# Exponent rows of the SSD heads by broadcast transfers instead of selection matmuls, with the clipped differences pinned in ScalarE's queue

## The chip, the core and the metric

The kernel runs on one core of a Trainium2 chip. Five engines work from queues of their own, each in the order in which its instructions were written: PE (TensorE, matmuls), DVE (VectorE), ACT (ScalarE), POOL (GpSimd) and SP (SyncE, which here only issues transfers). The metric is the device time of one execution in microseconds (us).

## The reference

A two-layer encoder on 512 tokens plus 16 meta tokens (L = 528 positions), width 2048, float32. The even layer is the one that matters here. Its input projection feeds 32 state-space (SSD) heads of width 64 in 8 groups, run forwards and backwards in chunks, and a convolution branch with 31 taps; both are gated and projected out. The odd layer is neighbourhood attention.

```
A_cs = jnp.cumsum(A, axis=2)
seg = A_cs[:, :, :, None] - A_cs[:, :, None, :]
Lmat = jnp.exp(jnp.where(tri, seg, -jnp.inf))
Y_diag = jnp.einsum("bclsgr,bcsgrp->bclgrp", CB[..., None] * Lmat, X)
Y_off = jnp.einsum("bclgn,bcgrpn->bclgrp", Cc, prev) * jnp.exp(A_cs)[..., None]
```

Per head and direction this needs, for every pair of positions in a chunk, the exponential of a difference of cumulative log decays, and for every position the exponential of the cumulative sum itself. The decays never exceed one, so the kernel writes the difference as the negative of a clipped one: exp(-relu(column - row)).

## The kernel before, in words

Positions lie along the free dimension and channels over the 128 partitions. A projection is 96 matmuls of 128x128 by 264 columns: 16 slices of the weights, three products (a high part and a low part of weights and of activations), two column halves. Weights come in halves of a panel, 512 KB each: SP issues the transfer (`raw`, three buffers), ACT splits off the high part (`wh`, L263, three buffers), DVE the low part (`wl`, L266), and PE uses the pair for 48 matmuls (L310). PE walks through the halves in a fixed order, so `wh` of a half can be written once PE has done with the half three back.

The even layer goes over 8 groups `g`. For each there are one or two convolution tiles (`glu_tile`), then six projections for B, C, two tiles of x and two of z. The SSD work of a group is a generator, `ssd`, which the loop pumps between the projections of the next group. Within `ssd` there are two passes `i`, each for two heads `j`:

- `T` (88 x 2 x 528, tag of two buffers) holds the clipped differences, then their exponentials (L611), then those times dt (L618) and times C·B (L619); the two directions are added at L621.
- `cq` (128 x 2 x 528, two buffers) holds the exponentials of the cumulative sums, then those times C (L612, L613).
- 64 matmuls into `py` (L640) read both `T` and both `cq` of the pass; DVE then makes the output y (L644, L645), and POOL writes it out (`yz_d`, L646).

To get one head's row of sums onto all partitions, PE multiplies a broadcast column of a selection matrix `sel` with `fhl`, the sums in a high and a low half (L605, two matmuls per head and direction into `pf` in PSUM). ACT reads `pf` six times for the clipped differences, one per chunk, with the chunk's column of sums as bias (L608), and once for the exponentials (L610). `pf`, `pc` and `py` share one PSUM slot of two banks (tag `big`).

A scheduler with a model of the engines' times places all instructions on the engines' queues; the `yield` numbers in `ssd` are costs that `step` takes off a budget of `SB_` = 7000 per step, and so set where in the program a piece of `ssd` is written.

Of the kernel before, what the change touches and what calls it, by code (L numbers as in the profile page):

```python
# [17 lines left out]
P = 128  # L18
# [65 lines left out]
def hybrid_encoder(ctx: ExitStack, tc: tile.TileContext, hT, win, wdt, wout, oin, oout, par, con,  # L84
# [24 lines left out]
    def cn(n):  # L109
        lo, hi = CON[n]  # L110
        return cst[:, lo:hi]
# [4 lines left out]
    def h2(ap):  # L116
        return ap.rearrange("p (a b) -> p a b", a=2)
# [2 lines left out]
        return h2(ap)[:, :, NB:]  # L120

    yz_d = dr.tile([KT, P, L], F32, name="yz_d")
    cv_d = dr.tile([KT, P, L], F32, name="cv_d")
    pt_d = dr.tile([KT, P, L], F32, name="pt_d")
    yb_d = dr.tile([KT, P, L], F32, name="yb_d")
# [255 lines left out]
    with ExitStack() as c0:  # L381
# [37 lines left out]
                if k >= 2:  # L419
                    nc.vector.tensor_tensor(ac, ac, raw, op=ALU.add)  # L420

        sel = cp.tile([P, 64], F32R, name="sel")
        nc.vector.tensor_copy(sel, cn("sel"))
        xp = [sp.tile([P, L + 4], F32, name=f"xp{i}") for i in range(2)]
        for t in xp:
            nc.gpsimd.memset(t[:, 0:2], 0.0)
# [93 lines left out]
        nc.gpsimd.memset(rf[:, ::CH], 0.0)  # L520
        nc.vector.tensor_tensor_scan(fc[0:32], rf[0:32], la[0:32], 0.0, ALU.mult, ALU.add)
        nc.vector.tensor_tensor_scan(fc[32:64, ::-1], rf[32:64], la[32:64, ::-1], 0.0, ALU.mult, ALU.add)
        fhl = dp.tile([P, L], F32R, name="fhl")
        nc.scalar.activation(fhl[:J], fc, AF.Copy)
        nc.vector.tensor_tensor(fhl[J:], fc, fhl[:J].bitcast(F32), op=ALU.subtract)
        fc3 = fc.rearrange("p (c t) -> p c t", c=NC)
        wd3 = wd.rearrange("p (c t) -> p c t", c=NC)
        nc.vector.tensor_tensor(wd3[0:32], fc3[0:32, :, CH - 1:CH].to_broadcast([32, NC, CH]), fc3[0:32], op=ALU.subtract)
# [20 lines left out]
            cols.append(t)  # L549
        fcol, dcol, wcol = cols  # L550

        def ssd(g, bT, cT, xs, zs):
            xb = sp.tile([CH, NC, 3 * P], F32, name="xb", tag="xb")
            pv = sp.tile([P, NC - 1, 2, 256], F32, name="pv", tag="pv")
            pc = psb.tile([P, 2, 512], F32, name="pc", tag="big")
# [38 lines left out]
            for i in range(2):  # L594
                gs, cs = [], []
                for j in range(2):
                    hl = 2 * i + j
                    hd = HPG * g + hl
                    T = sp.tile([CH, 2, L], F32, name="T", tag="T", bufs=2)
                    cq = sp.tile([P, 2, L], F32, name="cq", tag="cq", bufs=2)  # L600
                    for d in range(2):
                        pf = psb.tile([P, 2, 512], F32, name="pf", tag="big")
                        jj = d * NH + hd
                        for n in range(2):
                            nc.tensor.matmul(pf[:, n, :HL], sel[:, jj:jj + 1].to_broadcast([P, P]),  # L605
                                             fhl[:, n * HL:(n + 1) * HL], start=True, stop=True)
                        for c in range(NC):
                            nc.scalar.activation(T[:, d, c * CH:(c + 1) * CH], pf[:CH, c // 3, (c % 3) * CH:(c % 3 + 1) * CH],  # L608
                                                 AF.Relu, bias=fcol[:, c, d, hd:hd + 1], scale=-1.0)
                        nc.scalar.activation(h2(cq[:, d]), pf[:, :, :HL], AF.Exp)  # L610
                    nc.scalar.activation(T, T, AF.Exp, scale=-1.0)  # L611
                    nc.vector.tensor_tensor(cq[:, 0, CH:], cq[:, 0, CH:], cT[:, CH:], op=ALU.mult)  # L612
                    nc.vector.tensor_tensor(cq[:, 1, :L - CH], cq[:, 1, :L - CH], cT[:, :L - CH], op=ALU.mult)  # L613
                    yield 1050
                    for d in range(2):
                        for c in range(NC):
                            sl = slice(c * CH, (c + 1) * CH)
                            nc.scalar.activation(T[:, d, sl], T[:, d, sl], AF.Copy, scale=dcol[:, c, d, hd:hd + 1])  # L618
                        nc.vector.tensor_tensor(T[:, d], T[:, d], cbs[d], op=ALU.mult)  # L619
                    yield 1900  # L620
                    nc.vector.tensor_tensor(T[:, 0], T[:, 0], T[:, 1], op=ALU.add)  # L621
                    yield 650
                    gs.append(T)
                    cs.append(cq)
                py = psb.tile([P, 2, 512], F32, name="py", tag="big")
                for c in range(NC):
                    sl = slice(c * CH, (c + 1) * CH)
                    terms = [[], []]
                    for j in range(2):
                        hs = slice((2 * i + j) * HD, (2 * i + j + 1) * HD)  # L630
                        terms[j].append((xb[:, c, hs], gs[j][:, 0, sl]))
                        if c > 0:
                            terms[j].append((pv[:, c - 1, 0, hs], cs[j][:, 0, sl]))
                        if c < NC - 1:
                            terms[j].append((pv[:, NC - 2 - c, 1, hs], cs[j][:, 1, sl]))
                    nt = len(terms[0])
                    for q in range(nt):
                        for j in range(2):
                            a, b = terms[j][q]
                            nc.tensor.matmul(py[j * HD:(j + 1) * HD, c // 3, (c % 3) * CH:(c % 3 + 1) * CH], a, b,  # L640
                                             start=(q == 0), stop=(q == nt - 1))
                ti = 2 * g + i
                y = xs[i]
                nc.vector.scalar_tensor_tensor(h2(y), h2(y), pr("dd", ti, ti + 1), py[:, :, :HL], op0=ALU.mult, op1=ALU.add)  # L644
# [4 lines left out]
                else:  # L649
                    nc.scalar.activation(zs[i], y, AF.Square)  # L650
                    nc.vector.tensor_tensor(accy, accy, zs[i], op=ALU.add)
                yield 2100

        def step():
            pump(bgs, SB_)
# [974 lines left out]
```

## Time and profile before

| | |
|---|---|
| time, median of 3 runs | 2628.63 us (2628.37 to 2631.36) |
| profiled execution | 2629.41 us, span 2627.6 us |
| granted TensorE clock | 0.998 |
| SSD stretch in the span | about 140 to 1065 us |
| `pf` matmuls (L605) | 128 |
| `T` from `pf` on ACT (L608) | 384 |
| `cq` from `pf` on ACT (L610) | 64 |

The span runs from the first to the last instruction of the profiled execution. A busy PE in the page is not by itself a PE without gaps, since matmuls overlap; the distance from one start to the next tells more.

### The profile page before, as it was taken

How to read it: one execution, taken by the hardware profiler on the slowest of the kernel's cores; microseconds unless marked ns; L12 is line 12 of the kernel's file. 1: busy time of each engine (PE TensorE's matmuls, PEld its weight loads, DVE VectorE, ACT ScalarE, POOL GpSimd, SP SyncE). 2: the span in 40 equal slices, each digit the busy share in tenths (PEclk: the TensorE clock that was granted, in tenths of full speed). 3: DMA queues.
4: the chain of work that ended last, by engine and by line, in shares of the span. 5: the costliest groups of instructions: out<-in, count | busy, mean ns of one | idle time of the engine just before them, and what ended most of it. 6: DMA issues, size and time to landing. Idle time of an engine off the chain costs nothing.

```text
span 2627.6 us, 52699 instructions
## 1 busy us (share of the span) xinstructions
PE 2593.7 (99%) x21236; PEld 2480.7 (94%) x21236; DVE 2044.7 (78%) x3073; ACT 1421.8 (54%) x2654; POOL 335.8 (13%) x561
## 2 busy tenths in 40 slices
PE   8999999999999999999999999999999999999997
PEld 8999999999999999999999999999999987777797
DVE  6985967887686969997788888877777776666887
ACT  5366585666558566325554566644334355556543
POOL 0000000000000001100210311300000043434110
PEclk9999999999999999999999999999999999999999
DMA  4322223222222222533875876755555555544665
GB/s 174 100 74 94 81 77 95 82 95 73 94 85 74 89 91 90 175 107 104 274 231 164 300 219 208 258 161 161 156 161 146 151 143 139 135 120 130 224 186 159
DMA packets 163173, 373.28 MB, mean 142 GB/s; under 512 B 40896, under 2 KB 70784, under 8 KB 162928
## 3 DMA queue, kind: packets, MB, share of 16 engines
q1 hardware_dynamic: 137840, 289.96, 34.5%
q0 software_dynamic: 23072, 78.30, 11.2%
q8 instruction: 167, 2.74, 0.4%
q10 hardware_dynamic: 2016, 1.65, 0.2%
q14 instruction: 78, 0.64, 0.1%
HBM read 320.59 MB, written 49.25 MB: 141 GB/s over the span
## 4 chain that ended last, share of the span: by engine, by line
PE 87%; DVE 4%; ACT 4%; DMA 3%; issue 2%; POOL 0%; SPq 0%; DVEq 0%; ACTq 0%; POOLq 0%
PE ps L310 43%; PE pb L287 29%; PE ps L1192 6%; PE py L640 2%; PE po L1178 1%; PE st L580 1%; DVE a L454 1%; PE pq L1129 1%; DMA srt<-yb_d 1%; ACT T L608 1%; ACT L610 1%; DVE wl L266 1%; PE pa L1153 1%; DMA wy<-oout 1%; ACT wh L263 1%
## 5 line engine op out<-in xcount | busy, mean ns | idle before, releaser
L310 PE MATMUL ps<-rh,wh 128*128 128x264 f32 (+2 forms) x3520 | 730.3, 287 | 10.0 <-ACT rh L327 8.0
L310 PE MATMUL ps<-rh,wl 128*128 128x264 f32 (+2 forms) x3520 | 730.2, 287 | 0.0
L310 PE MATMUL ps<-rl,wh 128*128 128x264 f32 (+2 forms) x3520 | 725.6, 287 | 0.7 <-DVE rl L328 0.6
L263 ACT ACTIVATE wh<-raw 128x1024 fp32r<-128x1024 f32 (+1 forms) x349 | 368.9, 1057 | 525.3 <-PE ps L310 271.3
L310 PEld LDWEIGHTS ps<-rh,wh 128*128 128x128 f32 (+1 forms) x3520 | 549.2, 188 | 16.1 <-ACT rh L327 8.6
L266 DVE TENSOR_TENSOR wl<-raw,wh 128x1024 fp32r<-128x1024 f32 (+1 forms) x349 | 436.5, 1251 | 163.2 <-ACT wh L263 158.4
L310 PEld LDWEIGHTS ps<-rh,wl 128*128 128x128 f32 (+1 forms) x3520 | 548.9, 188 | 2.3 <-DVE wl L266 0.3
L310 PEld LDWEIGHTS ps<-rl,wh 128*128 128x128 f32 (+1 forms) x3520 | 546.5, 188 | 4.1 <-DVE rl L328 1.5
L287 PE MATMUL pb<-rh,wh 128*128 128x264 f32 (+1 forms) x1280 | 363.1, 284 | 3.3 <-DVE fo L1494 1.2
L287 PE MATMUL pb<-rl,wh 128*128 128x264 f32 (+1 forms) x1280 | 362.2, 283 | 0.0
L287 PE MATMUL pb<-rh,wl 128*128 128x264 f32 (+1 forms) x1280 | 361.8, 283 | 0.3 <-DVE wl L266 0.2
L454 DVE SCALAR_TENSOR_TENSOR a<-up,prm,a 128x528 f32<-128x528 f32 x464 | 342.9, 769 | 2.3 <-ACT a L449 0.9
L287 PEld LDWEIGHTS pb<-rh,wh 128*128 128x128 f32 x1280 | 241.1, 188 | 4.4 <-issue 1.7
L287 PEld LDWEIGHTS pb<-rh,wl 128*128 128x128 f32 x1280 | 240.3, 188 | 0.7 <-DVE wl L266 0.7
L287 PEld LDWEIGHTS pb<-rl,wh 128*128 128x128 f32 x1280 | 240.7, 188 | 0.0
L287 PE MATMUL pb<-ta,wh 128*128 128x264 f32 (+1 forms) x1280 | 234.5, 283 | 1.2 <-ACT wh L263 1.2
L287 PEld LDWEIGHTS pb<-ta,wh 128*128 128x128 f32 x1280 | 197.4, 188 | 1.6 <-ACT wh L263 1.6
L263 ACT ACTIVATE wh<-wy 128x1024 fp32r<-128x1024 f32 x109 | 115.6, 1060 | 136.4 <-PE pb L287 105.7
L287 PE MATMUL pb<-ta,wl 128*128 128x264 f32 (+1 forms) x640 | 181.1, 283 | 0.0
L266 DVE TENSOR_TENSOR wl<-wy,wh 128x1024 fp32r<-128x1024 f32 x109 | 133.4, 1223 | 50.6 <-ACT wh L263 50.4
L263 ACT ACTIVATE wh<-wb 128x1024 fp32r<-128x1024 f32 x80 | 84.7, 1059 | 102.2 <-PE pb L287 58.5
L287 PEld LDWEIGHTS pb<-ta,wl 128*128 128x128 f32 x640 | 120.2, 188 | 0.2 <-DVE wl L266 0.2
(389 smaller groups left out, 4096.4 us busy)
## 6 DMA issues: line engine op xcount, KB each, us to landing
raw<-win SPq DMA_DIRECT2D x192, 512.0 KB, 3.7
raw<-oin SPq DMA_DIRECT2D x84, 512.0 KB, 4.4
raw<-wout SPq DMA_DIRECT2D x40, 512.0 KB, 5.4
wb<-oin SPq DMA_DIRECT2D x22, 512.0 KB, 4.0
wy<-oin SPq DMA_DIRECT2D x22, 512.0 KB, 3.5
wy<-oin POOLq DMA_DIRECT2D x22, 512.0 KB, 8.1
raw<-oout SPq DMA_DIRECT2D x20, 512.0 KB, 4.8
srt<-h_d POOLq DMA_DIRECT2D x38, 264.0 KB, 5.4
```

The lines of the kernel that those rows point to most:

```text
L263: nc.scalar.activation(wh, raw, AF.Copy)
L266: nc.vector.tensor_tensor(wl, raw, wh.bitcast(F32), op=ALU.subtract)
L287: nc.tensor.matmul(acc, w[:, k, :], u[:, lo + o:lo + o + n], start=(new and k == 0 and j == 0), stop=(k == KH - 1 and j == 2), skip_group_ ...
L310: nc.tensor.matmul(ps[:M, n, :N], w[:, k, :], u[:, lo + n * HL:lo + n * HL + N], start=(kk == 0 and j == 0), stop=(kk == KT - 1 and j == 2))
L454: nc.vector.scalar_tensor_tensor(a, u[:, j:j + L], wv(j), a, op0=ALU.mult, op1=ALU.add)
L580: nc.tensor.matmul(st[:, :nd * 256], xb[:, c, 256:], xd[:, d0:d1].rearrange("p r x -> p (r x)"), start=True, stop=True)
L608: nc.scalar.activation(T[:, d, c * CH:(c + 1) * CH], pf[:CH, c // 3, (c % 3) * CH:(c % 3 + 1) * CH], AF.Relu, bias=fcol[:, c, d, hd:hd + 1 ...
L610: nc.scalar.activation(h2(cq[:, d]), pf[:, :, :HL], AF.Exp)
L640: nc.tensor.matmul(py[j * HD:(j + 1) * HD, c // 3, (c % 3) * CH:(c % 3 + 1) * CH], a, b, start=(q == 0), stop=(q == nt - 1))
L1129: nc.tensor.matmul(pqs[a, w][:, :n], x[hs, w * P:(w + 1) * P], y[hs, st:st + n], start=(j == 0), stop=(j == 2))
L1153: nc.tensor.transpose(pa[:, i * P:(i + 1) * P], sb[:, w, c:c + P], ident)
L1192: nc.tensor.matmul(h2(ps) if lo is None else ps, w[:, k, :], tok(u) if lo is None else u[:, lo:lo + S], start=(kk == 0 and j == 0), stop=( ...
```

## The change

The cumulative sums `fc` and their exponentials are written to a DRAM tile `f_d`, once each. A new function `rows` loads, for the two heads of a pass, both directions' rows with a partition step of 0: each of the 88 partitions of `T` and of the 128 partitions of `cq` gets a copy, `T` the sums and `cq` the exponentials. There are four such transfers a pass, 64 in all, on POOL's queue. Those of pass 0 are written at the start of a group's `ssd`, those of pass 1 just behind the `py` matmuls of pass 0. The clipped differences are then made in place in `T`, and each of these ACTIVATEs is tied behind the ACT instruction written before it. The selection matmuls, `sel`, `fhl` and the 64 exponentials of `cq` on ACT are gone. Pass 0 ends with two more yields of a whole step's budget each.

```diff
+    f_d = dr.tile([2, 2 * NH, L], F32, name="f_d")
...
-        sel = cp.tile([P, 64], F32R, name="sel")
-        nc.vector.tensor_copy(sel, cn("sel"))
...
-        fhl = dp.tile([P, L], F32R, name="fhl")
-        nc.scalar.activation(fhl[:J], fc, AF.Copy)
-        nc.vector.tensor_tensor(fhl[J:], fc, fhl[:J].bitcast(F32), op=ALU.subtract)
+        nc.gpsimd.dma_start(f_d[0], fc)
+        ef = e
+        nc.scalar.activation(ef, fc, AF.Exp)
+        nc.gpsimd.dma_start(f_d[1], ef)
...
+        def rows(g, i):
+            out = []
+            for j in range(2):
+                hd = HPG * g + 2 * i + j
+                T = sp.tile([CH, 2, L], F32, name="T", tag="T", bufs=2)
+                cq = sp.tile([P, 2, L], F32, name="cq", tag="cq", bufs=2)
+                for k, t in enumerate((T, cq)):
+                    s = f_d[k, hd]
+                    nc.gpsimd.dma_start(t, bass.AP(tensor=s.tensor, offset=s.offset,
+                                                   ap=[[0, t.shape[0]], [NH * L, 2], [1, L]]))
+                out.append((T, cq))
+            return out
+
         def ssd(g, bT, cT, xs, zs):
+            rw = rows(g, 0)
...
-                    T = sp.tile([CH, 2, L], F32, name="T", tag="T", bufs=2)
-                    cq = sp.tile([P, 2, L], F32, name="cq", tag="cq", bufs=2)
+                    T, cq = rw[j]
                     for d in range(2):
-                        pf = psb.tile([P, 2, 512], F32, name="pf", tag="big")
-                        jj = d * NH + hd
-                        for n in range(2):
-                            nc.tensor.matmul(pf[:, n, :HL], sel[:, jj:jj + 1].to_broadcast([P, P]),
-                                             fhl[:, n * HL:(n + 1) * HL], start=True, stop=True)
                         for c in range(NC):
-                            nc.scalar.activation(T[:, d, c * CH:(c + 1) * CH], pf[:CH, c // 3, (c % 3) * CH:(c % 3 + 1) * CH],
-                                                 AF.Relu, bias=fcol[:, c, d, hd:hd + 1], scale=-1.0)
-                        nc.scalar.activation(h2(cq[:, d]), pf[:, :, :HL], AF.Exp)
+                            sl = slice(c * CH, (c + 1) * CH)
+                            tc.keep_in_program_order(nc.scalar.activation(T[:, d, sl], T[:, d, sl], AF.Relu,
+                                                                          bias=fcol[:, c, d, hd:hd + 1], scale=-1.0))
...
+                if i == 0:
+                    rw = rows(g, 1)
...
                 yield 2100
+                if i == 0:
+                    yield SB_
+                    yield SB_
```

The scheduler places everything anew in the SSD stretch. Behind it the order of the engines' queues is, but for the last convolution taps and the work around them, the one of before, and SP's queue is the same throughout.

ACT's queue at pass 1 of group 1, before. `zt<-cv` is the square of the output y of pass 0, so it stands behind the pass's `py` matmuls; `wh` are weight halves.

```order
L650 ACTIVATE zt<-cv 128x528
L608 ACTIVATE T<-pf,fcol 88x88 x6
L610 ACT_TABLE_LOAD
L610 ACTIVATE cq<-pf 128x528
L688 ACT_TABLE_LOAD
L688 ACTIVATE zt<-zt 128x528
L263 ACTIVATE wh<-raw 128x1024
L608 ACTIVATE T<-pf,fcol 88x88 x6
L610 ACT_TABLE_LOAD
L610 ACTIVATE cq<-pf 128x528
```

The same place of ACT's queue now:

```order
L660 ACTIVATE zt<-cv 128x528
L617 ACTIVATE T<-T,fcol 88x88 x12
L701 ACTIVATE zt<-zt 128x528
L264 ACTIVATE wh<-raw 128x1024
L619 ACT_TABLE_LOAD
L619 ACTIVATE T<-T 88x1056
L626 ACTIVATE T<-T,dcol 88x88 x12
L617 ACTIVATE T<-T,fcol 88x88 x12
L264 ACTIVATE wh<-raw 128x1024
```

Twelve clipped differences of one head now stand together, ahead of the next weight half, and wait for a transfer where six of them waited for PE. The `cq` exponentials and two table loads are gone from the place.

POOL's queue from the output of pass 0 of group 0 on, before; `sg` is the gate of a convolution tile, `up` its zero borders, `cv_d` its result.

```order
L646 DMA yz_d<-cv 128x528
L663 TENSOR_TENSOR sg<-sg,rs_84 128x528
L646 DMA yz_d<-cv 128x528
L466 MEMSET up 128x15
L467 MEMSET up 128x15
L457 DMA cv_d<-a_3072 128x528
L646 DMA yz_d<-cv 128x528
```

And now:

```order
L656 DMA yz_d<-cv 128x528
L676 TENSOR_TENSOR sg<-sg,rs_85 128x528
L560 DMA T<-f_d 88x2x528 x2
L560 DMA cq<-f_d 128x2x528 x2
L656 DMA yz_d<-cv 128x528
L465 MEMSET up 128x15
L466 MEMSET up 128x15
L456 DMA cv_d<-a_3035 128x528
L560 DMA T<-f_d 88x2x528 x2
L560 DMA cq<-f_d 128x2x528 x2
L656 DMA yz_d<-cv 128x528
```

Ahead of each write of y now stand four row transfers, which need the same `py` matmuls to be over that y needs; the order of the others among themselves is unchanged.

DVE's queue at pass 1 of group 0, before, from the output y on:

```order
L645 TENSOR_TENSOR cv<-cv,zt 128x528
L687 TENSOR_TENSOR zt<-ps,rs_84 128x528
L266 TENSOR_TENSOR wl<-raw,wh 128x1024
L612 TENSOR_TENSOR cq<-cq,cv 128x440
L266 TENSOR_TENSOR wl<-raw,wh 128x1024
L613 TENSOR_TENSOR cq<-cq,cv 128x440
L619 TENSOR_TENSOR T<-T,cmu 88x528
```

And now:

```order
L655 TENSOR_TENSOR cv<-cv,zt 128x528
L700 TENSOR_TENSOR zt<-ps,rs_85 128x528
L620 TENSOR_TENSOR cq<-cq,cv 128x440
L621 TENSOR_TENSOR cq<-cq,cv 128x440
L620 TENSOR_TENSOR cq<-cq,cv 128x440
L621 TENSOR_TENSOR cq<-cq,cv 128x440
L267 TENSOR_TENSOR wl<-raw,wh 128x1024
```

The four products with `cq`, for both heads, moved together ahead of the next low part of the weights.

## The prediction

> **What bounds the kernel now.** First the page: which engine is busy, and is that the same in all stages? Then busy time by stretches: the SSD work, where every edit lies, and the tail of the convolution behind it.
>
> ```profile
> span 2627.6 us, 52699 instructions
> PE 2593.7 (99%) x21236; PEld 2480.7 (94%) x21236; DVE 2044.7 (78%) x3073; ACT 1421.8 (54%) x2654; POOL 335.8 (13%) x561
> 140.00:1065.00 925.00, 922.79 (x7989) 891.50 (x7988) 725.81 (x995) 589.09 (x1308) 41.03 (x62) 1.00 0.27 86
> 1065.00:1184.00 119.00, 119.00 (x981) 119.00 (x980) 112.38 (x149) 32.10 (x36) 12.91 (x23) 1.00 0.43 143
> ```
>
> The columns of the last two rows are the stretch, then busy time (and count) of PE, PEld, DVE, ACT and POOL, the clock, the DMA share and GB/s. In the SSD stretch PE is busy 922.8 of 925 us at full clock, DVE 78%, ACT 64%, the DMA engines 27%. A busy PE could still be one that waits inside, so the next view is its timeline, where starts can be subtracted, and then its waits.
>
> ```profile
> 332.56 0.28 PE L310 MATMUL ps<-rh,wl 128*128 128x264 f32 x1
> 332.68 0.41 PE L605 MATMUL pf<-fhl,sel 128*128 128x264 f32 x2
> 332.93 0.29 PE L310 MATMUL ps<-rh,wl 128*128 128x264 f32 x1
> 333.05 0.41 PE L310 MATMUL ps<-rh,wh 128*128 128x264 f32 x2
> 333.30 0.41 PE L310 MATMUL ps<-rl,wh 128*128 128x264 f32 x2
> ...
> PE pf L605 <- ACT cq L610: 1.4, 4, 0.4
> PE py L640 <- ACT cq L610: 0.6, 3, 0.3
> ```
>
> The matmuls start 0.12 us apart (332.56, 332.68; two selection matmuls from 332.68 to 332.93), and a selection matmul takes the same slot as a projection's. PE waits 2.0 us in all in that stretch. So PE sets the pace there, with nothing between its instructions: an instruction taken from it shortens the stretch, unless another engine then comes too late.
>
> **The change part by part.** *Selection matmuls removed.* These are the groups of the stretch that the change touches (busy time, mean ns of one, idle before):
>
> ```profile
> L605 PE MATMUL pf<-fhl,sel 128*128 128x264 f32 x128 | 27.0, 292 | 1.4 <-ACT cq L610 1.4
> L608 ACT ACTIVATE T<-pf,fcol 88x88 f32<-88x88 f32 x384 | 91.8, 335 | 19.8 <-PE pf L605 19.7
> L618 ACT ACTIVATE T<-T,dcol 88x88 f32<-88x88 f32 x384 | 103.4, 371 | 0.5
> L610 ACT ACTIVATE cq<-pf 128x528 f32<-128x528 f32 x64 | 39.9, 624 | 0.3
> ```
>
> The 292 ns are a latency; the slot is 0.25 us for two. 64 pairs x 0.245 us = 15.7 us off PE. The 1.4 us in which `pf` waited for ACT to empty the shared PSUM slot go too: 17.1 us. The 0.6 us at `py` I leave in.
>
> *ACT.* 64 exponentials go, 39.9 us. The 384 clipped differences stay but read SBUF in place of PSUM. The nearest row of that kind, L618, has 371 ns against 335: 384 x 0.036 = 14 us more busy at most, and none at least if the operand's place is not the reason. Either way ACT, 64% busy, loses work, and pays PE nothing for it, since PE was not waiting for it.
>
> The Trainium skill (page "ScalarE: Activation LUTs", section "Step-by-step: what each stage is for") says that ScalarE is placed nearer to PSUM and slower towards SBUF. It speaks of destinations, and would point the way the two rows do, against this edit; by either the sum of PE's path stays.
>
> *DVE* loses two operations ahead of the stretch; the four `cq` products of a pass now stand together. It gains nothing else.
>
> *Transfers added.* Each of 64 row transfers is issued by POOL; 32 carry 88 x 4,224 bytes = 372 KB, 32 carry 128 x 4,224 = 541 KB, together 29 MB in some 905 us, 32 GB/s beside 86. None like them stands in the trace (every partition reads the same row). The nearest are plain reads issued by POOL, and the group of the weights shows what they share the engines with:
>
> ```profile
> L708 POOL DMA_DIRECT2D srt<-h_d x38: 536/538/852, 1573.6 to 1690.4; - x38
> DMA to landing us min/median/max: 2.9/5.3/11.6
> ...
> wy<-oin POOLq DMA_DIRECT2D x22, 512.0 KB, 8.1
> raw<-win SPq DMA_DIRECT2D x192, 512.0 KB, 3.7
> ```
>
> The second row is for the 264 KB transfers of that line. POOL's part, 0.54 us each, is 35 us more on an engine with 41 of 925 busy: covered. Landing of `T`: between the 264 KB median 5.3 and the 512 KB of 8.1 (which also adds), 372 KB come to 5.3 + 0.44 x 2.8 = 6.5 us from issue; bounds 2.9 and 11.6. I take 6.5. The share of the DMA engines goes from 27% to about 27 x (86 + 32) / 86 = 37%; weights are fetched into three buffers, so about two halves ahead, 2 x 48 x 0.122 = 11.7 us of PE's work against 3.7: they stay covered.
>
> *The new wait, and who stands behind it.* In pass 0 the rows are asked for when the `py` matmuls of the group before have read the old `T`; from the chain of waits and ACT's timeline:
>
> ```profile
> 246.19 2.59 PE py L640 x62
> 257.95 1.41 ACT L608 ACTIVATE T<-pf,fcol 88x88 f32<-88x88 f32 x6
> ```
>
> From 248.8 to 257.95 are 9.1 us, more than 6.5: no wait there. In pass 1 the rows can be asked for only behind the `py` matmuls of pass 0, and the pinned differences stand right behind y's square on ACT. Group 1 in the timeline (PE, ACT, DVE):
>
> ```profile
> 324.30 0.32 PE L640 MATMUL py<-cq,pv 128*64 128x88 f32 x4
> 326.23 0.63 ACT L650 ACTIVATE zt<-cv 128x528 f32<-128x528 f32 x1
> 328.39 1.44 ACT L608 ACTIVATE T<-pf,fcol 88x88 f32<-88x88 f32 x6 [1.53 <-PE pf L605]
> 333.60 1.04 ACT L263 ACTIVATE wh<-raw 128x1024 fp32r<-128x1024 f32 x1
> 337.28 0.61 ACT L610 ACTIVATE cq<-pf 128x528 f32<-128x528 f32 x1
> 337.79 1.08 ACT L611 ACTIVATE T<-T 88x1056 f32<-88x1056 f32 x1
> 338.90 3.22 ACT L618 ACTIVATE T<-T,dcol 88x88 f32<-88x88 f32 x12
> 342.02 1.05 ACT L263 ACTIVATE wh<-raw 128x1024 fp32r<-128x1024 f32 x1
> 343.52 1.22 DVE L266 TENSOR_TENSOR wl<-raw,wh 128x1024 fp32r<-128x1024 f32 x1
> 344.14 0.41 PE L310 MATMUL ps<-rh,wh 128*128 128x264 f32 x2
> 351.19 0.51 PE L310 MATMUL ps<-rh,wh 128*128 128x264 f32 x2
> ```
>
> ACT now: `py` ends at 324.6, rows land at 324.7 + 6.5 = 331.2 (2.8 us later than the 328.39 at which ACT went on before). Twelve differences at L618's spacing, 3.2 us, to 334.4; the gate's 0.65 to 335.0; the weight half to 336.1, low part to 337.3. PE needs it at 344.14, less the selection pairs (three at 0.245) and the wait (0.5) that go ahead of it, so at 342.9: 5.6 us in hand. Then a table load (335.99 to 337.28 before, 1.3), exponentials 1.1, products 3.2, the second head's differences 3.2, and the next half: 336.1 + 8.8 + 1.05 = 345.9, low part to 347.1. PE needs that one at 351.19, less four pairs and the wait, so at 349.7: 2.6 us in hand. So PE does not notice rows that land within 6.5 + 2.6 = 9.1 us of `py`'s end. What is late next if they do is this second weight half.
>
> The Trainium skill (page "DMA: Bandwidth & Descriptors", section "Anatomy of one DMA — SWDGE (gpsimd) path") gives a GpSimd transfer about 2.0 us plus its bytes at 436 GB/s. By it `T` would land an estimated 2.9 us after issue, and the sum would be the bare 17.1. The rows above are all longer, so the bounds go by them.
>
> *Sum.* 15.7 + 1.4 = 17.1 off the span, 1 us kept back for waits of `py` on the later `T` (three such waits made 0.6 before): 2627.6 - 16.1 = 2611.5 span. The profiled execution took 2629.41, the median of the runs is 2628.63; so the time comes to 2628.6 - 16.1 = **2612.5 us**.
>
> **Rivals.** *Rows too late (slower).* Each of the 8 pass-1 places costs PE what the landing exceeds 9.1 us by. Over 9.1 + 17/8 = 11.2 us the gain is gone. At 13.5 us it is 8 x 4.4 = 35 us: 2628.6 - 17 + 35 = 2647. For it: the maximum of 11.6 above, four transfers of 1.8 MB at once, all partitions reading one row. Against: that maximum is from a stretch with more DMA load than the 27% here, and `T` is issued ahead of `cq`.
>
> *The gain is given back behind the stretch (no change).* PE comes to the sum over the convolution results early and DVE does not:
>
> ```profile
> L462 DVE TENSOR_TENSOR accl<-accl,a x15: 692/701/709, 204.0 to 1183.4; 128x528 f32<-128x528 f32 x15
> L335 PE MATMUL cs<-accl,cst x4: 384/386/386, 1190.1 to 1190.7; 128*128 128x264 f32 x4
> L454 DVE SCALAR_TENSOR_TENSOR a<-up,prm,a x464: 662/758/1830, 60.1 to 1181.8; 128x528 f32<-128x528 f32 x155
> ```
>
> DVE ended at 1184.1, 6 us before PE asked. By the order of DVE's queue 357 of the 464 taps stand ahead of the 160th weight half, where 362 stood before: five more for the tail, 5 x 0.76 = 3.8 us. If DVE gained no time in the stretch, PE would ask 16 us earlier and wait 16 + 3.8 - 6 = 14: 2612.5 + 14 = 2626. For it: 112.4 of 119 us busy in the tail. Against: DVE's taps are interleaved with the weights' low parts and so move up with PE, and it has 199 us idle in the stretch to do it in.
>
> *ACT's relief counts too.* If PE's pace held hidden waits for ACT, the gain would be larger; the even 0.12 us starts speak against, and the row of 2.0 us caps it. It ends within 2 us of the forecast.
>
> **How the numbers follow.** Forecast 0.80, the last rival included; gain given back 0.11; rows too late 0.09. A measurement of this kernel tells 0.2% (5.3 us) from no change: faster means below 2623.4. The forecast is faster; of the given-back case 0.02 still is, 0.09 is not; late rows I count as slower. Faster 0.82, same 0.09, slower 0.09. Range: at the low end all 17.1 us and the rest of the waits, with DVE and ACT freer, up to 22: 2606; at the high end rows that land at 10.9 us on the median, 8 x 1.8 = 14, or the given-back case: 2626. Within it about 0.88. The forecast's own range is 2608 to 2618.
>
> **What would show it.** No L605 row; the stretch between the first and last `py` of the groups shorter by 16 us; PE's starts still 0.12 us apart. The wait of `T` in ACT's rows named for DMA `T<-f_d` in place of PE `pf`, 2 to 4 us a group in pass 1, near none in pass 0. `T<-f_d` landing at 5 to 8 us. No PE wait on `wh` or `wl` in the stretch, and L335 without a wait. I am wrong if PE waits for ACT `wh` behind the pass-1 differences, if the rows land beyond 9.1 us, or if L335 waits for DVE.

## The result: slower, by 0.37%

| | before | changed |
|---|---|---|
| median | 2628.5 us | 2638.4 us (2634.2 to 2642.5) |
| ratio, 95% interval | | 1.0037 (1.0023 to 1.0051) |
| profiled execution, span | 2627.6 us | 2634.5 us |

The forecast was 2612.5 us. The profile of the changed kernel, first its page's head and the rows of stretches (columns as in the prediction):

```profile
span 2634.5 us, 52449 instructions
PE 2582.3 (98%) x21108; PEld 2469.2 (94%) x21108; DVE 2039.9 (77%) x3071; ACT 1385.0 (53%) x2576; POOL 382.4 (15%) x627
140.00:1065.00 925.00, 904.53 (x7769) 873.29 (x7770) 709.44 (x978) 548.41 (x1225) 81.24 (x118) 0.99 0.36 114
1065.00:1184.00 119.00, 119.00 (x1018) 118.89 (x1014) 115.11 (x152) 35.19 (x39) 15.45 (x26) 1.00 0.44 151
```

The 128 selection matmuls are gone (21236 to 21108), and yet the same stretch of 925 us holds less work than before: PE is busy 904.5 us of it, not 922.8, and the clock has left 1.00. The tail behind is unchanged. PE's waits in that stretch (total, times, longest):

```profile
PE st L594 <- DVE xd L589: 6.2, 3, 3.1
PE ps L311 <- DVE sg L674: 5.2, 3, 1.8
PE py L648 <- DVE T L629: 4.6, 7, 0.9
PE pt L584 <- ACT cv L441: 3.2, 1, 3.2
PE ps L311 <- DVE wl L267: 1.3, 1, 1.3
```

20.5 us, where there were 2.2 (925 us less PE's busy time, 904.53 and 922.79); 17.3 of them are for DVE and 3.2 for ACT. What DVE and ACT wait for, from their waits and the page's list of DMA issues (KB, median us to landing):

```profile
DVE cq L620 <- DMA cq<-f_d: 64.6, 22, 6.6
...
ACT T L617 <- DMA T<-f_d: 37.7, 8, 11.5
...
cq<-f_d POOLq DMA_DIRECT2D x32, 528.0 KB, 8.6
T<-f_d POOLq DMA_DIRECT2D x32, 363.0 KB, 6.2
```

One of these places, at the start of group 2's `ssd`, in POOL's, DVE's and PE's timelines:

```profile
353.52 1.32 POOL L676 TENSOR_TENSOR sg<-sg,rs 128x528 f32<-128x528 f32 x1 [25.06 <-ACT sg L675]
354.79 1.54 POOL L560 DMA_DIRECT2D T<-f_d  x2
356.32 1.48 POOL L560 DMA_DIRECT2D cq<-f_d  x2
...
358.43 0.69 DVE L576 TENSOR_TENSOR cml<-pc,cst 88x528 f32<-88x528 f32 x1
363.83 0.62 DVE L620 TENSOR_TENSOR cq<-cq,cv 128x440 f32<-128x440 f32 x1 [4.71 <-DMA cq<-f_d]
364.37 0.61 DVE L621 TENSOR_TENSOR cq<-cq,cv 128x440 f32<-128x440 f32 x1
364.90 0.68 DVE L589 TENSOR_TENSOR xd<-xb,wcol 88x512 f32<-88x512 f32 x1
...
362.25 0.28 PE L311 MATMUL ps<-rh,wh 128*128 128x264 f32 x1
365.63 1.52 PE L594 MATMUL st<-xd,xb 88*128 88x512 f32 x2 [3.10 <-DVE xd L589]
...
368.25 0.64 PE L311 MATMUL ps<-rh,wl 128*128 128x264 f32 x2
368.69 0.64 PE L311 MATMUL ps<-rh,wh 128*128 128x264 f32 x2
...
370.09 0.40 PE L311 MATMUL ps<-rl,wh 128*128 128x264 f32 x2
370.33 0.40 PE L311 MATMUL ps<-rh,wl 128*128 128x264 f32 x2
```

DVE stands 4.7 us at a `cq` product whose row is on its way; behind it stands `xd`, and PE needs `xd` at 362.5. This is a pass 0, for which the prediction said "no wait there": ACT indeed waits for no `T` in a pass 0, but DVE does wait for `cq`. The rows were also asked for 2.3 us after the end of the last `py` matmul (352.45), behind the gate product `sg` in POOL's queue. The other long wait for `xd`, 2.87 us at 835.6, is of the same kind in group 6, with rows asked for 2.9 us late.

And then something that no part of the prediction had: from 366.2 to 369.6 two matmuls take 0.44 us from start to start in place of 0.24. The trace's record of the granted clock has 0.5 there, and twice more in the stretch, each time for 3.4 us; before, it had none there. The stretch around the second:

```profile
711.00:714.40 3.40, 3.40 (x18) 3.40 (x17) 1.72 (x2) 1.99 (x3) 1.30 (x1) 0.50 0.25 58
```

The waits for the gate product `sg` and for `cv` have another source. Group 0 and group 3, pass 1:

```profile
239.63 0.70 DVE L627 TENSOR_TENSOR T<-T,cmu 88x528 f32<-88x528 f32 x1 [1.26 <-ACT T L626]
240.26 0.70 DVE L674 TENSOR_TENSOR sg<-ps,rs 128x528 f32<-128x528 f32 x1
241.10 0.48 PE L311 MATMUL ps<-rh,wh 128*128 128x264 f32 x2 [1.58 <-DVE sg L674]
...
556.44 3.22 ACT L617 ACTIVATE T<-T,fcol 88x88 f32<-88x88 f32 x12 [8.57 <-DMA T<-f_d]
575.21 0.64 ACT L441 ACTIVATE cv<-cv 128x528 f32<-128x528 f32 x1
575.90 0.31 PE L584 MATMUL pt<-cst,cv 128*88 128x128 f32 x1 [3.17 <-ACT cv L441]
```

In the first, DVE stands at a product of `T` for which ACT is late, and the gate product stands behind it. In the second, ACT works without a pause from the end of its wait for `T` to the `cv` that PE stands at. Both hang on the `T` rows, through ACT.

**Bookkeeping.** From the prediction's own terms: -15.7 for the matmuls, -2.2 for the waits of before, +20.5 for the new ones, + half of 10.2 us at half clock: +7.7. Where the last SSD work is over (the 158th weight half, at 1073 us) PE is 7.0 us behind the kernel before. So the matmuls' gain is there, and waits and clock eat more than all of it.

### The profile page after: what moved, and what is told of

Same layout as the page of the kernel before. It is cut to its first block, busy times and chain, and to the rows that moved or that the text cites. A ratio compares the mean times of both kernels' runs of the same rounds, so it can differ in the third digit from the quotient of the medians.

```text
span 2634.5 us, 52449 instructions
## 1 busy us (share of the span) xinstructions
PE 2582.3 (98%) x21108; PEld 2469.2 (94%) x21108; DVE 2039.9 (77%) x3071; ACT 1385.0 (53%) x2576; POOL 382.4 (15%) x627
## 4 chain that ended last, share of the span: by engine, by line
PE 76%; ACT 8%; DMA 6%; issue 5%; DVE 4%; POOL 1%; SPq 0%; DVEq 0%; POOLq 0%; ACTq 0%
PE ps L311 34%; PE pb L288 28%; PE ps L1205 7%; ACT T L617 2%; PE po L1191 2%; DMA T<-f_d 2%; ACT T L626 2%; ACT wh L264 1%; PE py L648 1%; PE st L594 1%; DVE wl L267 1%; PE pq L1142 1%; DMA cq<-f_d 1%; DVE a L453 1%; ACT T L619 1%
## 5 line engine op out<-in xcount | busy, mean ns | idle before, releaser
L311 PEld LDWEIGHTS ps<-rh,wh 128*128 128x128 f32 (+1 forms) x3520 | 549.7, 189 | 19.7 <-ACT rh L328 8.8
L453 DVE SCALAR_TENSOR_TENSOR a<-up,prm,a 128x528 f32<-128x528 f32 x464 | 337.6, 765 | 16.3 <-ACT a L448 15.6
L617 ACT ACTIVATE T<-T,fcol 88x88 f32<-88x88 f32 x384 | 102.8, 354 | 37.7 <-DMA T<-f_d 37.7
```

Source lines behind the costliest of these rows:

```text
L311: nc.tensor.matmul(ps[:M, n, :N], w[:, k, :], u[:, lo + n * HL:lo + n * HL + N], start=(kk == 0 and j == 0), stop=(kk == KT - 1 and j == 2))
L453: nc.vector.scalar_tensor_tensor(a, u[:, j:j + L], wv(j), a, op0=ALU.mult, op1=ALU.add)
L617: tc.keep_in_program_order(nc.scalar.activation(T[:, d, sl], T[:, d, sl], AF.Relu, bias=fcol[:, c, d, hd:hd + 1], scale=-1.0))
```

## Experiments

All times stand against runs of the kernel before on the same chip (medians 2627.6 to 2629.3). In the diffs, `...` leaves out what only follows.

### What the selection matmuls and the rows are worth

`e1`, on the kernel before:

```diff
-                        for n in range(2):
+                        for n in (0, 1, 0, 1):
```

> The kernel before, with every pair of selection matmuls done twice into the same bank (128 more matmuls; what is computed stays the same). It prices the selection matmuls by themselves, with no rows and no transfers. Theory of the prediction (they lie on the path of a TensorE that paces this stretch): 64 pairs by 0.245 us = 15.7 us slower, about 2644 us, and nothing else moves. Rival (the selection matmuls lay in the shadow of some other wait and were never worth 15.7 us): within 5 us of the kernel before.

2644.5 us, ratio 1.0060 (1.0048 to 1.0072). 128 matmuls more cost 16 us: the first theory's number, so the term of 15.7 us stands.

`e6`, on the changed kernel:

```diff
-                    nc.gpsimd.dma_start(t, bass.AP(tensor=s.tensor, ...
...
-        tc.keep_in_program_order(nc.scalar.activation(T[:, d, sl], T[:, d, sl], AF.Relu,
+        tc.keep_in_program_order(nc.scalar.activation(T[:, d, sl], rs0[:CH, sl], AF.Relu,
...
-        nc.vector.tensor_tensor(cq[:, 0, CH:], cq[:, 0, CH:], cT[:, CH:], op=ALU.mult)
+        nc.vector.tensor_tensor(cq[:, 0, CH:], rs0[:, CH:], cT[:, CH:], op=ALU.mult)
```

> The changed kernel with no transfer of rows at all: the differences of T and the products of cq read a tile that has long been there (rs0) in the place of the rows. This leaves out the spreading of each head's own exponents, so the values are not those of the model; the count of arithmetic instructions on every engine is that of the changed kernel. It bounds what the removal of the selection matmuls is worth without any late row. Theories A and B (all the loss is time in which some engine waits for rows): about 2611 us, 2606 to 2616. Theory C (the freed matmuls were never worth 15.7 us, or the new order on TensorE costs by itself): 2622 or more.

2616.1 us, 0.9951 (0.9939 to 0.9963): at the edge of what theories A and B said. PE's only waits left in the stretch:

```profile
PE py L639 <- DVE T L620: 4.7, 5, 1.0
```

So the loss hangs on the rows; and even with no row to wait for, `py` now waits for `T`, which it hardly did before.

### Which wait: the cq products or the T rows

`e4` moves the `cq` products, `e2` gives the `cq` rows of pass 1 tiles of their own, `e3` the `T` rows:

```diff
-                    nc.vector.tensor_tensor(cq[:, 0, CH:], cq[:, 0, CH:], cT[:, CH:], op=ALU.mult)
...
                     nc.vector.tensor_tensor(T[:, 0], T[:, 0], T[:, 1], op=ALU.add)
+                    tc.keep_in_program_order(nc.vector.tensor_tensor(cq[:, 0, CH:], cq[:, 0, CH:], cT[:, CH:], op=ALU.mult))
...
```

```diff
+                if k == 0 and i == 1:          # e2: k == 1
+                    t = [rsa[:n], extra] if j else [tp.tile([P, L], F32, name="own", tag="st", bufs=2)[:n] for _ in range(2)]
...
+            own = rows(g, 1, 0)                # at the start of ssd; e2: rows(g, 1, 1)
```

> The changed kernel, with the two cq by C products of each head moved in VectorE's order from ahead of the T products to behind the sum of T, and pinned there. Theory A (the loss comes from VectorE, which stands at the cq rows for 66.8 us in all, with the product xd, the GLU product of L674 and the T products behind it): the waits of TensorE on xd, on the GLU product and on T shrink from 20 us to some 10 or less, and the kernel takes 2618 to 2628 us, faster than the changed one by 10 us or more; VectorE's wait for cq falls under 15 us. What is then left is ScalarE's wait for the T rows. Theory B (the loss comes from ScalarE, whose pinned differences wait 37.7 us for the T rows): VectorE's wait moves from the cq products to the T products, and the time stays within 4 us of the changed kernel's 2638. Theory C (the transfers themselves or the missing matmuls cost, not who waits for them): no change.

> The changed kernel, with tiles of their own for the cq rows of the second pass, asked for at the start of the group; the T rows stay as in the changed kernel. VectorE's wait at the cq products (66.8 us in the changed kernel) should fall below 15 us, while ScalarE goes on waiting some 40 us for T. Theory A (VectorE's blocked queue makes the loss): 2626 or less. Theory B (ScalarE's wait for T makes it): 2634 or more. Theory D, formed after the run that only moved the cq products (2635.6): the two waits lie side by side in the same few microseconds behind the first pass's py products, so taking one away only lets the other decide: 2633 to 2637, like that run.

> The changed kernel, with tiles of their own for the T rows of the second pass, asked for at the start of the group; the cq rows and the place of their products stay as in the changed kernel. ScalarE's wait for T should be gone. Theory B: 2620 or less. Theory A: about the changed kernel's 2638, with VectorE's wait at cq as long as before or longer, since it reaches these products sooner. Theory D (side by side): 2632 to 2638.

| | time, us | ratio (95%) |
|---|---|---|
| `e4` cq products late | 2635.6 | 1.0028 (1.0016 to 1.0039) |
| `e2` cq rows own | 2638.1 | 1.0027 (1.0015 to 1.0039) |
| `e3` T rows own | 2629.7 | 1.0000 (0.9989 to 1.0011) |

PE's waits in the stretch, first `e4`, then `e3`:

```profile
PE ps L311 <- DVE sg L674: 9.1, 5, 2.4
PE py L648 <- DVE T L627: 8.5, 8, 2.1
```

```profile
PE ps L311 <- DVE zt L709: 7.5, 2, 3.8
PE st L602 <- DVE xd L597: 2.6, 4, 0.7
PE ps L311 <- DVE wl L267: 0.3, 1, 0.3
```

In `e4` DVE no longer stands at `cq` at all and `xd`'s waits are gone, as theory A said, but the waits for the gate product and for `T` grew by as much. Theory A falls as the whole cause.

In `e2` DVE's wait at `cq` fell to 29 us only, not under 15, and ACT's for `T` stayed at 36; the time is that of the changed kernel, as B said. But `e2` did not take the wait away: DVE stands 24 us more at the rows in the own tiles. Eight of the products, all of group 0, are over by 144 us, so that the `cq` row it stands at up to 227.1 us, for 6.4 us, is one of group 1's first pass, asked for as soon as its tile came free and put into the same place. So the unchanged time of `e2` says little against A.

In `e3` (where, as in all runs with own tiles, an exponential is split in two and a row of these tiles is a transfer by itself) ACT no longer waits, and half of PE's waits went, those for `sg`, `py` and `cv` among them: more than A or D said, and not to B's 2620. So `xd`'s waits go with the `cq` rows (`e4`), the others with the `T` rows (`e3`).

Either edit leaves a wait that takes the other's place, so three ways of taking both away at once:

```diff
# e5: e3 and e4 together
# e9: as e5, the cq products of both heads directly ahead of py
+                for cq in cs:
+                    tc.keep_in_program_order(nc.vector.tensor_tensor(cq[0][:, CH:], cq[0][:, CH:], cT[:, CH:], op=ALU.mult))
...
# e11: the four spare tiles go to T and cq of the first head of pass 1; cq products as in e4
+                if i == 1 and j == 0:
+                    t = [rsa, extra] if k else [tp.tile(...) for _ in range(2)]
```

> The changed kernel with two edits. The cq by C products stand behind the sum of T, as in the run with that edit alone; and the T rows of the second pass have tiles of their own (two of the tail's buffers, one free row buffer and one new tile), so that their transfers are asked for at the start of the group and are there long before ScalarE reaches them. ScalarE's exponential of T is split into one per direction, 32 more instructions. Theories A and B both expect that the waits are gone and the gain of the matmuls shows: 2628.6 - 17 = about 2611 us, 2608 to 2618. Theory C (the price lies in the transfers or in the schedule, not in waits for rows) expects 2630 or more.

> As the run with T rows of their own and the cq products behind the sum of T, but with the cq products of both heads at the very end of the pass, directly ahead of the py products that need them. In that run (2632.5 us) VectorE still stood up to 6.3 us at the first head's cq product, with the GLU and z products behind it, and TensorE waited 8.0 us for those. Theory D: with neither engine standing at rows that are on their way, TensorE's waits fall to about the 4.7 us of the run without rows, and the time comes to 2616 to 2624 us, faster than the kernel before. If the transfers cost by themselves, or the order of the scheduler does, it stays at 2630 or more.

> The same four spare row buffers shared out in another way: T and cq of the second pass's first head have tiles of their own, asked for at the start of the group; the second head's rows are asked for when the first pass's py products free their tiles, and the cq products stand behind the sum of T. The second head's rows have some 8 us more than the first head's before they are used, about their landing time of 6 to 9 us. Theory D: 2616 to 2624, as with the cq products at the end of the pass. Theory C (transfers cost by themselves): 2630 or more.

`e5` 2632.5 us, 1.0017 (1.0009 to 1.0026); `e9` 2630.7, 1.0001 (0.9990 to 1.0011); `e11` 2638.1, 1.0028 (1.0018 to 1.0037). All missed: none came near 2620, and PE still waited 13.7, 16.1 and 16.1 us in the stretch. So late rows are not the whole of it. What these runs and `e6` share is found in PE's order.

### Where the py products stand

The kernel before and the changed one at pass 1 of group 0, from PE's and DVE's timelines: end of pass 0's `py`, sum of the first head's `T`, first `py` of pass 1.

```profile
214.31 0.32 PE L640 MATMUL py<-cq,pv 128*64 128x88 f32 x4
...
230.08 0.71 DVE L621 TENSOR_TENSOR T<-T 88x528 f32<-88x528 f32 x1
...
239.82 0.36 PE L640 MATMUL py<-T,xb 88*64 88x88 f32 x2
```

```profile
215.99 0.32 PE L648 MATMUL py<-cq,pv 128*64 128x88 f32 x4
...
222.09 3.22 ACT L617 ACTIVATE T<-T,fcol 88x88 f32<-88x88 f32 x12 [2.77 <-DMA T<-f_d]
...
232.69 0.70 DVE L629 TENSOR_TENSOR T<-T 88x528 f32<-88x528 f32 x1
...
233.54 0.34 PE L648 MATMUL py<-T,xb 88*64 88x88 f32 x2 [0.73 <-DVE T L629]
```

From the start of the `py` row of pass 0 to the sum's end are 16.5 us before and 17.4 now: the rows hardly lengthened the chain. But its reader stood 25.5 us behind pass 0 and now stands 17.6 behind. Medians over the eight groups, from the same rows (the last column is the median of the eight differences):

| | first sum ready, us | first `py`, us | slack, us |
|---|---|---|---|
| before | 19.2 | 26.1 | 6.8 |
| changed | 17.7 | 17.8 | 0.2 |
| `e6` no rows | 11.8 | 13.9 | 2.1 |
| `e3` T rows own | 5.7 | 8.1 | 2.2 |

In `e5`, `e9` and `e11` the slack is 2.7, 2.4 and 2.7 us. In `e6` the second sum, at 23.5 us, has the rest of the `py` products 0.1 us behind it. It looks as if the scheduler puts the products where it takes `T` to be ready: in the rows of the table each change that shortens the chain moves them nearer. Hence theory E, and its test, which writes them later:

```diff
+                if i == 1:
+                    yield SB_
+                    yield SB_
+                    yield SB_
                 py = psb.tile([P, 2, 512], F32, name="py", tag="big")
```

`e12` is the changed kernel with it, `e13` is `e3` with it.

> The changed kernel with three more yields of a step ahead of the py products of the second pass, and nothing else: the rows, their buffers and the cq products stay. In the changed kernel the scheduler put the first of these py products 16 us of TensorE's work behind those of the first pass, where the kernel before had 25 us, while the chain that feeds them (rows, differences, exponentials, products on VectorE, sum) took about as long as before, 17 us; here the first one stands 22 us behind. Theory E (what the change spends is the slack in TensorE's order: the scheduler takes the rows as landed sooner than they land and puts their readers too early): the waits of py on T (4.6 us) fall under 1 us, those on the GLU product shrink, and the time falls by 5 us or more against the changed kernel, to 2625 to 2633; what is left are xd's waits behind the cq products, 6 us. Theory B alone (ScalarE late, wherever py stands): no change against 2638. Theory C (transfers): no change.

> T rows of the second pass in tiles of their own (2629.7 us by itself), and three more yields ahead of that pass's py products. With the own tiles alone the scheduler had moved the first of these products to 7 us behind the first pass, and VectorE stood 36 us at the cq rows; TensorE's waits came to 10.4 us and the granted clock fell to half for 10 us in all. Theory E: the products stand 22 us behind, the waits on z and xd fall to 4 us or less, no clock drop in the stretch, and the time is 2616 to 2622, faster than the kernel before. If the own tiles had brought all that there is to bring: 2628 to 2632.

`e12`: 2632.9 us, 1.0012 (1.0002 to 1.0021), slack 7.3 us. `e13`: **2618.4 us, 0.9965 (0.9952 to 0.9978)**, slack 13.2 us: faster than the kernel before by about 9 us at that ratio, than the changed one by 20. PE's waits, `e12` first:

```profile
PE st L594 <- DVE xd L589: 8.2, 3, 3.3
PE ps L311 <- DVE sg L678: 5.3, 2, 2.9
PE ps L311 <- DVE wl L267: 1.5, 2, 1.0
PE py L652 <- DVE T L629: 1.1, 2, 0.6
```

```profile
PE ps L311 <- DVE zt L713: 3.9, 1, 3.9
PE st L602 <- DVE xd L597: 3.8, 4, 2.0
```

`e12` shows theory E's part by itself: `py`'s waits go from 4.6 to 1.1 us, but the waits for `xd` and `sg` stay (those for `sg` had been expected to shrink). With the `T` rows early as well, PE waits 7.8 us and the clock halves once, for 6.8 us; the time is as expected, though no halving and less of waits had been. B's part (8.7 us with own tiles) and E's (5.5) make 20 together, more than their sum; `sg`'s waits, which `e12` keeps, are gone in `e13`.

### The other two parts of the change

`e7` takes the tie off the differences, `e8` the two yields behind pass 0:

```diff
-                            tc.keep_in_program_order(nc.scalar.activation(T[:, d, sl], T[:, d, sl], AF.Relu,
-                                                                          bias=fcol[:, c, d, hd:hd + 1], scale=-1.0))
+                            nc.scalar.activation(T[:, d, sl], T[:, d, sl], AF.Relu,
+                                                 bias=fcol[:, c, d, hd:hd + 1], scale=-1.0)
# e8
-                if i == 0:
-                    yield SB_
-                    yield SB_
```

> The changed kernel without the tie of the clipped differences to their place on ScalarE; everything else as it is. The scheduler then puts the first py products of the second pass 21 us behind those of the first, not 16. Theory E: the waits of py on T fall, as with the yields; but the differences may now stand further ahead on ScalarE and hold up what is behind them for longer. 2628 to 2640. If the tie is what costs, under 2628.

> The changed kernel without the two yields behind the first pass. The scheduler then puts the first py products of the second pass 21 us behind those of the first, and the others 25 us. Theory E: fewer waits of py on T, 2630 to 2636. If these yields give the rows the time to land, as the only thing they can be for, ScalarE's wait for T (37.7 us) grows and the kernel is slower than the changed one: 2640 or more.

`e7`: 2666.3 us, 1.0149 (1.0134 to 1.0164). `e8`: 2662.5 us, 1.0126 (1.0109 to 1.0143). Both far slower, against what theory E said of them: `py` does stand further off (25.3 and 25.7 us), but the first sum is ready only at 25.1 and 25.6 us, so the slack is as small as in the changed kernel. The distance alone says nothing; it is the distance less the chain that counts. But slack is the smaller part here: PE waits 37 and 35 us in the stretch, and `py` has 11 and 8 of them. In `e7` 25.0 us are waits for `xd`, at the start of a group, where ACT now waits for `T` as well (15 waits for `T` in the stretch, not 8); in `e8` 9.2 are for ACT's `wh` and 8.4 for `xd`. This suggests that without the tie the differences of a pass 0 come too early on ACT and hold it up. `e8`'s other number (2640 or more) held, though not by its reason: ACT's wait for `T` did not grow, it is 30.8 us against 37.7. So the tie is worth some 28 us to this way of loading rows, and the yields 24; how the yields do it is not worked out here.

### What is left

`e14`, `e15` and `e16` are `e5`, `e4` and `e9` with the three yields of `e12`; `e17` is `e6` with them.

> The changed kernel with the cq products behind the sum of T (2635.6 us by itself) and three more yields ahead of the second pass's py products (2632.9 by itself); buffers and transfers as in the changed kernel. If the two waits add up (xd's 6 to 8 us go with the first edit, py's with the second), 2618 to 2626. If ScalarE's wait for T is what is left in any order (theory B), 2630 to 2636.

> T rows of the second pass in tiles of their own, py products later (together 2618.4 us), and the cq products behind the sum of T. If the 3.9 us of xd's waits and the 3.9 us of z's wait that were left there come from VectorE standing at the cq rows: 2610 to 2615, at or under the run without any rows (2616.1). If they come from VectorE's own work (739 us busy in the stretch of 925): 2617 to 2621.

> The same, with the cq products of both heads at the end of the pass, behind the yields and directly ahead of the py products. By the same reading 2610 to 2615 if waits for the cq rows are what is left; 2617 to 2624 if the place ahead of py makes py wait for VectorE in their stead.

> The kernel without any transfer of rows (which leaves out the spreading of each head's own exponents: differences and cq products read a tile that has long been there), with three more yields ahead of the second pass's py products. If the missing matmuls are worth the 17 us that the prediction gave them, and the nearness of the py products cost the run without rows its 4.7 us, it comes to 2609 to 2613 us; the distance to 2618.4 is then what the rows still cost in the best kernel. If TensorE's order has nothing to do with it, 2616 as without the yields.

| | time, us | ratio (95%) |
|---|---|---|
| `e15` cq products late, py later | 2631.5 | 1.0008 (0.9997 to 1.0018) |
| `e14` and T rows own | 2618.5 | 0.9962 (0.9947 to 0.9977) |
| `e16` cq products at the end | 2629.2 | 1.0003 (0.9993 to 1.0012) |
| `e17` no rows, py later | 2614.6 | 0.9943 (0.9927 to 0.9960) |

`e15` against `e14`: with both edits of the order, 13 us still lie in ScalarE's wait for `T`, that is in the time at which the rows are asked for, as the second of `e15`'s expectations had it. `e14` against `e13`: where the `cq` products stand is then worth nothing; the time lies in the range that its expectation gave to DVE's own work, though which work it is was not looked at. `e16` missed both of its own; it is slow with only 10.8 us of waits; the sum of its waits and its clock gives a stretch 5.4 us shorter than before, and it is 0.5 shorter. Why, no run tells.

`e17` missed its number by 1.6 us. At the end of the SSD work PE is 17.4 us ahead of the kernel before, which looks like the prediction's 17.1 for the matmuls and the old waits. It is so by luck: PE still waits 3.0 us for `T` there and the clock halves once (1.7 us), so that the terms give 13.2, and 4.2 us come from elsewhere, from where no run tells. With all its transfers `e13` is within 4 to 6 us of `e17` (by the times and by the ratios), so theory C, that the transfers cost by themselves, does not explain the changed kernel's loss.

In the two profiles `e17` ends 15.0 us ahead (spans of 2627.6 and 2612.6), in the medians 13. The waits behind the stretch, before and `e17`:

```profile
PE ps L310 <- ACT rh L324: 1.8, 1, 1.8
```

```profile
PE ps L311 <- ACT rh L325: 3.2, 1, 3.2
```

At some 1455 to 1470 us PE waits for the high part of a projection's input, 1.4 us longer when it comes earlier, and the clock halves behind that pause. The lead falls to 14.5 us there, but shorter waits behind it bring it back: it is 17.4 again by 1670 us. What is lost for good goes at 2420 us, where the clock halves behind the wait for `sb` (1.6 us), and within the 100 us behind it (0.8).

## Why the prediction was wrong

**Right:** PE sets the pace, and the matmuls are worth 15.7 us (`e1`: 16). `T` lands 6.2 us from issue in the median, 6.5 were said (6.4, had the sum counted `T` as 363 KB, as the rows do). ACT waits for `T` 2.3 to 3.4 us in six of the eight passes 1, as said, but 8.6 and 11.5 us in the other two, and in no pass 0. A clipped difference from SBUF takes 354 ns, between the bounds of 335 and 371. The weight halves all but hold: PE waits 1.3 us for a low part, once. L335 does not wait, so that rival is out. The DMA share is 36% (37% said). POOL's issue takes 0.75 to 0.77 us, not 0.54, and is covered all the same. The Trainium skill's figure that the prediction quoted gave an estimated 2.9 us to landing; the measured 6.2 decides.

**The step that failed** is the list of who stands behind the new waits, and with it the term "1 us kept back for waits of `py` on the later `T`". The waits came to 20.5 us. Three parts of the working made it so small:

*On DVE*, "the four `cq` products of a pass now stand together. It gains nothing else." The order of DVE's queue shown ahead of the prediction has the four together behind the pass's output. They read the third and fourth transfer of a pass, which land 8.6 us from issue; ACT's wait for the first was priced and this one was not. DVE waits 64.6 us there. What PE misses by it is `xd` (6.2 us), in passes 0, where "no wait there" was said: `e4`, in which DVE does not stand at `cq`, has no wait for `xd`.

*On ACT*, "PE does not notice rows that land within 6.5 + 2.6 = 9.1 us" and "What is late next if they do is this second weight half." The row that ACT waits for landed 5.0 to 9.0 us behind `py`'s end in the eight passes 1, all within the 9.1, and PE did notice: not by the weight half, which had room, but by the gate product (5.2 us), `py` (4.6) and once `cv` (3.2), which had none. All three are gone in `e3`, in which ACT does not wait.

*On PE*, the place of `py` was taken from the old order. It had moved 8 us nearer, so 6.8 us of slack had gone before the first row was late.

**The rival "rows too late"** had the right sign by the wrong road: it let PE lose only beyond a landing of 9.1 us, and by the weight half.

**In none of the cases:** the clock. The 20.5 us of waits cost another 5.1 us (three times 3.4 at half speed).

The same sum, -15.7 - 2.2 + waits + half of the time at half clock, against PE's place at the end of the SSD work, in us:

| | waits | at half clock | sum | measured |
|---|---|---|---|---|
| changed | 20.5 | 10.2 | +7.7 | +7.0 |
| `e2` | 19.7 | 10.2 | +6.9 | +7.5 |
| `e4` | 17.7 | 6.8 | +3.2 | +5.2 |
| `e5` | 13.7 | 13.7 | +2.7 | +3.0 |
| `e3` | 10.4 | 10.2 | -2.4 | -3.4 |
| `e11` | 16.1 | 20.5 | +8.5 | +8.7 |
| `e12` | 16.2 | 20.5 | +8.5 | +5.3 |
| `e13` | 7.8 | 6.8 | -6.7 | -12.1 |
| `e6` | 4.7 | 0 | -13.2 | -15.4 |

It holds within some 2 us but for `e12` (3 us) and `e13` (5 us); of the runs not in the table `e9` and `e15` fit within 2, `e14` ends 3 us earlier than it gives, `e17`, `e7` and `e8` 4 to 7 earlier, `e16` 5 later. So it carries the changed kernel's loss; what else a rearranged order brings or takes, up to some 6 us, stays open.

## What to carry to other kernels

When a wait moves from one engine to another, price every engine that waits for the new source, the last transfer as well as the first, and list what stands behind each waiting instruction. Where a scheduler places the readers, take their distance from the chain that feeds them anew from the changed order: work that is shortened on paper pulls its readers nearer, and slack can go without any duration growing. And a gain on a saturated TensorE shows only as far as the engines that feed it keep their time ahead.

## What the runs showed of the hardware

TensorE's clock can halve after a pause of some 2 us. In the 18 traces, the pauses of PE between 140 and 2500 us with no other pause of 0.6 us or more within 9 us, and those of them that a stretch at half clock followed within 8 us (a pause is the distance of two starts less the usual one):

| pause, us | pauses | followed by half clock |
|---|---|---|
| 0.6 to 1.5 | 65 | 0 |
| 1.5 to 2.0 | 21 | 2 |
| 2.0 to 2.5 | 32 | 13 |
| 2.5 to 3.0 | 11 | 7 |
| 3.0 to 3.5 | 12 | 11 |
| over 3.5 | 16 | 16 |

Each of these stretches at half clock lasts 3.4 us or a multiple, and within one trace all begin on one grid: in the changed kernel at 366.2, 711.0, 837.3 and 2622.4 us, which are 101.0, 138.0 and 661.0 times 3.4133 us apart from the first. The same pause can pass or cost 1.7 us more, by where it lies on the grid. The wait for `sb` between 2415 and 2475 us, 1.9 us idle in every trace, was followed by half clock in 9 of the 18. In these nine it ended 1.80 to 3.20 us behind a point of the grid, and so lay in one period but for 0.1 us at most. In the other nine it ended 0.09 to 1.61 us behind one, with 0.3 us or more ahead of the point.

That suggests counting PE's idle time by grid period (pauses over 0.15 us, from the end of one matmul in the trace to the start of the next). Over 140 to 2500 us the 18 traces have 12365 periods at full clock:

| idle in the period, us | periods | next period at half clock |
|---|---|---|
| under 1.70 | 12294 | 0 |
| 1.70 to 1.90 | 19 | 11 |
| over 1.90 | 52 | 52 |

So in this kernel the clock halves when PE has been idle for about half of a period (1.7 to 1.9 of 3.41 us); the ends of matmuls are modelled in the trace, which may be why the border is not sharp. The Trainium skill (page "TensorE: Matmul & The Clock Gate", section "Part 1: The HAM clock gate") describes a free-running window of 3413 ns that decides the clock; the grid agrees. Its rule to have no idle gaps over some 3.4 us (section "HAM oscillation — how this bites in real kernels") is too mild here by these counts: from 2 us on a pause can be enough.
